# Head sums, centring and lora products of an RWKV-7 block: split F32R products in place of plain F32 ones

## The chip, the cores and the metric

The kernel runs on one core of a Trainium2 chip. The metric is the device time of one execution in microseconds. The page's names of the engines are used: PE is TensorE (PEld its weight loads), DVE is VectorE, ACT is ScalarE, POOL is GpSimd, SP is SyncE, whose queue issues most of the loads.

## The reference

One decoder block for 512 tokens of width 2048, batch 1, depth 1, all in float32. An adaLN-modulated RMS norm is projected by `w_in`; 1024 columns go to 16 RWKV-7 heads of 64, 1024 to a causal pooling mixer; both are joined by `w_out`, and a gated MLP with a causal convolution follows. The change is in the RWKV part:

```python
    r, k, v, xw, xa, xg = jnp.split(p, list(RWKV_SPLITS), axis=-1)     # p = p + mu * (shifted p - p)
    w = -jax.nn.softplus(-(w0 + jnp.tanh(xw) @ w2)) - 0.5               # lora, 64 wide
    a = jax.nn.sigmoid(a0 + xa @ a2)                                    # lora, 64 wide
    g = jax.nn.sigmoid(xg) @ g2                                         # gate, 160 wide
    kk = heads(k * k_k)
    kk = kk / jnp.maximum(jnp.sqrt(jnp.sum(kk * kk, axis=-1, keepdims=True)), L2_EPS)   # sum over a head
    k = k * (1.0 + (a - 1.0) * k_a)
    y = _wkv7_scan(r_h, decay, k_h, v_h, -kk, kk * a_h)                 # S = S*w + (S a) b + v k ; y = S r
    mean = jnp.mean(y, axis=-1, keepdims=True)                          # over a head
    var = jnp.mean(jnp.square(y - mean), axis=-1, keepdims=True)
    y = (y - mean) * lax.rsqrt(var + GN_EPS) * ln_w + ln_b
    bonus = jnp.sum(r_h * k_h * r_k, axis=-1, keepdims=True) * v_h      # sum over a head
    return (y + bonus) * g
```

## The kernel before

Features lie on the 128 partitions and the 512 tokens along the free dimension. The large products are split: a float32 operand x becomes `hi`, its value cast to F32R, and `lo = x - hi`, also F32R; `mm3` makes hi·hi + hi·lo + lo·hi out of three F32R products (L120 to L122). The cast is made by ScalarE and the subtraction by VectorE (`split_weights`, L113 and L115; `wsplit`, L855 and L857).

The stages: modulation and the first eight column tiles of `w_in` (tile `pf`); the recurrence; `w_out`; the MLP. In the recurrence the 16 heads are taken as 8 pairs of 128 partitions, and 512 tokens as 4 chunks of 128. For each pair there are three parts. `stage_a` makes decay and rates from the lora weights (L375, L376), a running sum along the tokens (a scan, L383), the norm of k (squares L397, head sum L399), the matrix of a chunk and part of its inverse (by VectorE, through DRAM), and the bonus (head sum L460, L462). `stage_b` finishes the inverse, as `y1` (upper rows) and `y2`. `stage_c` runs over the four chunks with the state `sbd`; in each, `R` is made (L553), then `U` out of `y1`, `y2` and `R` (L556 to L559); after the chunks come centring (L590, matrix `cent`), the variance (L594, `bmean`), the norm and the gate product (L602, L603). `bones`, `bmean` and `cent` are three constant 128x128 matrices in `hmat`; a product with one of them sums or averages over the 64 partitions of each head. All these products were plain F32.

Around them stand products that nobody waits for soon: `win_pair(p + 2)` projects r, k, v two pairs ahead (tile `mm`, 3 x 48 products, the results go to DRAM through `spill`), and `ada_rest` has VectorE multiply rows of `w_ada` (`war`, L351, 192 in all) for the later modulation.

The order on each engine is made by a scheduler from priorities (`hp()` puts the recurrence first) and free buffers of the pools; each engine then works its list in that order, and waits where something is not ready. A tile that has a tag takes one of the `bufs` buffers of that tag: `ring` has 7, `war` 3, `post` 2, `spill` 2.

Of the kernel before, what the change touches and what calls it, by code (L numbers as in the profile page):

```python
# [9 lines left out]
F32 = mybir.dt.float32  # L10
# [6 lines left out]
P = 128  # L17
T = 512
# [37 lines left out]
def block_kernel(ctx, tc, a, out, stop=None, dbg=None):  # L56
# [14 lines left out]
    hmat = tp.tile([P, 3, P], F32, tag="hmat", name="hmat")  # L71
    nc.sync.dma_start(hmat, a["cmat"][:, 2:5, :])
# [6 lines left out]
    scanm = tp.tile([P, NC, 129], F32, tag="scanm", name="scanm")  # L79
    nc.gpsimd.memset(scanm, 1.0)  # L80
    nc.gpsimd.memset(scanm[:, :, 0:1], 0.0)
    lanei = tp.tile([64, 16, 16], F32, tag="lanei", name="lanei")
    nc.sync.dma_start(lanei, a["lanei"][:, :, :])
# [93 lines left out]
    if True:  # L177
# [53 lines left out]
        if True:  # L231
# [5 lines left out]
            def ring(name):  # L237
                return ring16(name)[:, 16:]

            def ring16(name):  # L240
                return ra.tile([P, 16 + T], F32, tag="ring", name=name, bufs=7)


            xwa = ra.tile([P, T], F32, tag="xwa", name="xwa")
            xg1 = ra.tile([P, T], F32, tag="xg1", name="xg1")
            xg2 = ra.tile([P, T], F32, tag="xg2", name="xg2")
# [18 lines left out]
            S.activation(xg2, xg2, AF.Sigmoid)  # L265
# [67 lines left out]
    y1 = ra.tile([P, 8, 64], F32, tag="y1", name="y1")  # L333
    G.memset(y1[64:128], 0.0)
# [25 lines left out]
    def r8(t, n=64):  # L360
        return t[:, 0 : 8 * n].rearrange("p (s j) -> p s j", s=8)
# [3 lines left out]

    def stage_a(p, rkv):
        q = Pair()
        r, k, v = rkv
        lw = q.lw = ra.tile([P, 3, P], F32, tag="lw", name="lw", bufs=2)
        nc.sync.dma_start(lw, a["lora"][p, :, :, :])  # L370
# [4 lines left out]
        PE.matmul(psw, lw[0:64, 0, :], xwa[0:64, :], start=True, stop=True)  # L375
        PE.matmul(psal, lw[64:128, 0, :], xwa[64:128, :], start=True, stop=True)  # L376
# [6 lines left out]
        V.tensor_tensor_scan(cs[:, :, :].rearrange("p c t -> p (c t)"), scanm[:, :, :].rearrange("p c t -> p (c t)"),  # L383
                             sg[:, :, :].rearrange("p c t -> p (c t)"), 0.0, op0=ALU.mult, op1=ALU.add)
# [14 lines left out]
        PE.matmul(psn, bones, sq, start=True, stop=True)  # L399
# [868 lines left out]
```

## Time and profile before

| | |
|---|---|
| time, median of 3 runs | 2369.44 us (2361.89 to 2372.39) |
| profiled execution | 2368.65 us, its span 2366.9 us |
| busy: PE, DVE, ACT | 95%, 69%, 45% of the span |
| mean granted TensorE clock | 0.991 |
| recurrence | about 150 to 790 us of the span |

In the rows of the trace a shape such as "128*64" after the names is the part of TensorE's array that the instruction uses, in rows and columns, and "128x512 f32" is the output and its type; F32R operands are shown as f32 in products, and as fp32r in casts. Ends of products are modelled, so starts are what to compare. The page's digits are busy tenths of a slice of 1/40 of the span.

### The profile page before, as it was taken

To read this page: it belongs to the slowest core of one execution; us is meant where nothing else is said; L and a number is where in the kernel's file an instruction comes from. 1 tells how busy PE (TensorE), PEld (TensorE's weight loads), DVE (VectorE), ACT (ScalarE), POOL (GpSimd) and SP (SyncE) were. 2 spreads that over 40 slices of the span, in tenths; PEclk is the share of its full clock that TensorE was granted. 3 is DMA by queue.
4 is the path that set the end of the run, shared out by engine and by line. 5 is a ranking of instruction groups with operands and counts; after the bars stand their busy time and mean duration, and the time that the engine had idled before them with its cause. 6 is when DMAs were issued, how large, how long until landed. Compare 5 with 4: busy or idle time off the path is not lost.

```text
span 2366.9 us, 42831 instructions
## 1 busy us (share of the span) xinstructions
PE 2256.6 (95%) x17122; PEld 1960.0 (83%) x17122; DVE 1636.4 (69%) x2591; ACT 1067.4 (45%) x1501; POOL 126.0 (5%) x185
## 2 busy tenths in 40 slices
PE   3878999999999999999999999999999999999997
PEld 2655666666676789999999999999999888888897
DVE  6987677777765556788888877777777645353454
ACT  3235344445433345655555555555555522233353
POOL 0000000000000000010101000000000000110000
PEclk9999999999999999999999999999999999999998
DMA  9976655566655766598888877777776767664464
GB/s 340 339 227 181 165 151 157 156 171 178 164 143 154 268 199 192 178 282 250 227 246 233 243 208 199 198 197 199 199 197 186 237 213 269 228 209 118 123 185 156
DMA packets 226234, 483.06 MB, mean 204 GB/s; under 512 B 74545, under 2 KB 79601, under 8 KB 217841
## 3 DMA queue, kind: packets, MB, share of 16 engines
q1 hardware_dynamic: 206114, 413.21, 54.7%
q0 software_dynamic: 18864, 66.07, 13.6%
q8 instruction: 134, 2.20, 0.4%
q10 hardware_dynamic: 1056, 1.05, 0.1%
q14 instruction: 66, 0.54, 0.1%
HBM read 441.70 MB, written 38.54 MB: 203 GB/s over the span
## 4 chain that ended last, share of the span: by engine, by line
PE 75%; issue 10%; DVE 7%; DMA 4%; ACT 3%; SPq 1%; POOL 0%; POOLq 0%; DVEq 0%; ACTq 0%
PE b L122 18%; PE b L120 18%; PE b L121 18%; PE mm L121 4%; PE mm L122 4%; PE mm L120 4%; DVE jk L212 3%; DMA war<-ada 1%; PE pb L541 1%; PE pb L539 1%; DVE wlo L115 1%; DMA wrow<-wup 1%; DMA rkv<-sp 1%; PE pa L298 1%; DMA wraw<-wout 1%
## 5 line engine op out<-in xcount | busy, mean ns | idle before, releaser
L122 PE MATMUL b<-t,ulo 128*128 128x256 f32 x1408 | 397.2, 282 | 0.0
L120 PE MATMUL b<-t,uhi 128*128 128x256 f32 x1408 | 396.8, 282 | 0.0
L121 PE MATMUL b<-t,uhi 128*128 128x256 f32 x1408 | 396.7, 282 | 0.0
L122 PE MATMUL b<-act,ulo 128*128 128x512 f32 (+1 forms) x880 | 308.0, 350 | 0.0
L121 PE MATMUL b<-act,uhi 128*128 128x512 f32 (+1 forms) x880 | 307.8, 350 | 0.0
L120 PE MATMUL b<-act,uhi 128*128 128x512 f32 (+1 forms) x880 | 307.7, 350 | 0.0
L120 PE MATMUL b<-y,uhi 128*128 128x256 f32 x1056 | 298.1, 282 | 2.6 <-ACT uhi L855 2.6
L122 PE MATMUL b<-y,ulo 128*128 128x256 f32 x1056 | 297.6, 282 | 0.6 <-DVE ulo L857 0.6
L121 PE MATMUL b<-y,uhi 128*128 128x256 f32 x1056 | 297.8, 282 | 0.0
L857 DVE TENSOR_TENSOR ulo<-wd,uhi 128x1024 fp32r<-128x1024 f32 (+1 forms) x120 | 136.3, 1136 | 215.9 <-ACT uhi L855 206.7
L120 PEld LDWEIGHTS b<-t,uhi 128*128 128x128 f32 x1408 | 266.9, 190 | 0.0
L122 PEld LDWEIGHTS b<-t,ulo 128*128 128x128 f32 x1408 | 266.9, 190 | 0.0
L121 PEld LDWEIGHTS b<-t,uhi 128*128 128x128 f32 x1408 | 266.8, 190 | 0.0
L113 ACT CAST whi<-wraw 128x512 fp32r<-128x512 f32 x236 | 144.9, 618 | 265.0 <-PE mm L121 117.1
L855 ACT CAST uhi<-wquart 128x1024 fp32r<-128x1024 f32 x156 | 163.8, 1050 | 203.8 <-PE b L121 177.5
L855 ACT CAST uhi<-wd 128x1024 fp32r<-128x1024 f32 (+1 forms) x120 | 117.3, 978 | 290.8 <-PE b L121 290.2
L857 DVE TENSOR_TENSOR ulo<-wquart,uhi 128x1024 fp32r<-128x1024 f32 x156 | 190.8, 1224 | 72.0 <-ACT uhi L855 72.0
L115 DVE TENSOR_TENSOR wlo<-wraw,whi 128x512 fp32r<-128x512 f32 x236 | 161.0, 687 | 88.6 <-ACT whi L113 81.6
L855 ACT CAST uhi<-r 128x1024 fp32r<-128x1024 f32 x132 | 138.6, 1050 | 163.7 <-PE b L121 162.2
L857 DVE TENSOR_TENSOR ulo<-r,uhi 128x1024 fp32r<-128x1024 f32 x132 | 161.2, 1221 | 62.4 <-ACT uhi L855 62.4
L120 PEld LDWEIGHTS b<-y,uhi 128*128 128x128 f32 x1056 | 200.2, 190 | 3.0 <-ACT uhi L855 3.0
L122 PEld LDWEIGHTS b<-y,ulo 128*128 128x128 f32 x1056 | 200.0, 189 | 0.8 <-DVE ulo L857 0.8
(315 smaller groups left out, 4699.1 us busy)
## 6 DMA issues: line engine op xcount, KB each, us to landing
wquart<-wup SPq DMA_DIRECT2D x176, 512.0 KB, 4.8
wa<-ada SPq DMA_DIRECT2D x48, 1024.0 KB, 7.1
war<-ada SPq DMA_DIRECT2D x192, 256.0 KB, 3.6
wd<-wdn SPq DMA_DIRECT2D x80, 512.0 KB, 3.9
wraw<-win SPq DMA_DIRECT2D x140, 256.0 KB, 4.0
wraw<-wout SPq DMA_DIRECT2D x96, 256.0 KB, 3.7
wquart<-wup POOLq DMA_DIRECT2D x44, 512.0 KB, 7.5
r<-wup SPq DMA_DIRECT2D x44, 512.0 KB, 4.4
```

The lines of the kernel that those rows point to most:

```text
L113: S.copy(hi, raw)
L115: eng.tensor_tensor(lo, raw, hi[:, :].bitcast(F32), op=ALU.subtract)
L120: PE.matmul(ps, wh, xh, start=start, stop=False, skip_group_check=more)
L121: PE.matmul(ps, wh, xl, start=False, stop=False, skip_group_check=more)
L122: return PE.matmul(ps, wl, xh, start=False, stop=stop, skip_group_check=more)
L212: V.scalar_tensor_tensor(jk, wa, 1.0, cb, op0=ALU.mult, op1=ALU.mult, accum_out=mod[:, j : j + 1])
L298: PE.matmul(ps, pw[:, i, d * P : (d + 1) * P], zs[i], start=i == 0, stop=i == 1)
L539: PE.matmul(pss[:, h, 0:128], bt[HS[h], cl], ar[HS[h], c, 1, :], start=True, stop=True)
L541: PE.matmul(pss[:, h, 128:384], kt[HS[h], cl], ar[HS[h], c, :, :], start=True, stop=True)
L855: S.copy(hi[:, 0:n], src)
L857: lo_of[0] = V.tensor_tensor(lo[:, 0:n], src, hi[:, 0:n].bitcast(F32), op=ALU.subtract)
```

## The change

The four head sums and the centring per pair become products of a split operand: `head_sums` casts its operand to `hi`, subtracts for `lo` and adds the two F32R products with the same constant matrix; `hmat` is cast to F32R once. (`y` is split likewise, ahead of `cent`.) The two lora products become three F32R products each, of split weights (`lsplit`) and a split `xwa`; the gate product becomes five, of which the last two hold the 32 columns that are left of `g2`: `xg3` keeps hi and lo of xg2 in two groups of 32 partitions, and the packed weights repeat theirs.

To make room, the scan along 516 columns becomes four of 129 without its mask `scanm`; `y1`, `x5`, `nl`, `lanei` and `xyl` share two tiles, `half1` and `half2`, the first two on partitions 0 to 63 and the others on 64 to 127; `y1` has no zero rows below it any more, and its product reads `R[0:64]`. `sqy` takes the buffer of `Tm`, the lora weights one of `war`, `xwa` and `xg1` those of `spill`, `xg2` one of `post`.

```diff
@@
     nc.sync.dma_start(cmat, a["cmat"][:, 0:2, :])
-    hmat = tp.tile([P, 3, P], F32, tag="hmat", name="hmat")
-    nc.sync.dma_start(hmat, a["cmat"][:, 2:5, :])
+
+    hmat = tp.tile([P, 3, P], F32R, tag="hmat", name="hmat")
+    hraw = wp.tile([P, WC], F32, tag="wraw", name="hraw", bufs=4)[:, 0 : 3 * P]
+    nc.sync.dma_start(hraw, a["cmat"][:, 2:5, :].rearrange("p i j -> p (i j)"))
+    S.copy(hmat[:, :, :].rearrange("p i j -> p (i j)"), hraw)
     ident, ones = (cmat[:, i, :] for i in range(2))
@@
     nc.sync.dma_start(mlev, a["mlev"][:, :, :])
-    scanm = tp.tile([P, NC, 129], F32, tag="scanm", name="scanm")
-    nc.gpsimd.memset(scanm, 1.0)
-    nc.gpsimd.memset(scanm[:, :, 0:1], 0.0)
-    lanei = tp.tile([64, 16, 16], F32, tag="lanei", name="lanei")
-    nc.sync.dma_start(lanei, a["lanei"][:, :, :])
     prec = tp.tile([P, 16], F32, tag="prec", name="prec")
@@
-            def ring(name):
-                return ring16(name)[:, 16:]
+            def ring(name, dt=F32):
+                return ring16(name, dt)[:, 16:]
-            def ring16(name):
-                return ra.tile([P, 16 + T], F32, tag="ring", name=name, bufs=7)
+            def ring16(name, dt=F32):
+                return ra.tile([P, 16 + T], dt, tag="ring", name=name, bufs=7)
-            xwa = ra.tile([P, T], F32, tag="xwa", name="xwa")
-            xg1 = ra.tile([P, T], F32, tag="xg1", name="xg1")
-            xg2 = ra.tile([P, T], F32, tag="xg2", name="xg2")
+            xwa = ra.tile([P, T], F32, tag="spill", name="xwa", bufs=2)
+            xg1 = ra.tile([P, T], F32, tag="spill", name="xg1", bufs=2)
+            xg2 = ra.tile([P, T], F32, tag="post", name="xg2", bufs=2)
             for i, t in enumerate((xwa, xg1, xg2)):
@@
             S.activation(xg1, xg1, AF.Sigmoid)
-            S.activation(xg2, xg2, AF.Sigmoid)
+            S.activation(xg2[0:64], xg2[0:64], AF.Sigmoid)
+
+            def split_in(t, name):
+                hi = ra.tile([P, T], F32R, tag=name + "h", name=name + "h")
+                lo = ra.tile([P, T], F32R, tag=name + "l", name=name + "l")
+                S.copy(hi, t)
+                V.tensor_tensor(lo, t, hi[:, :].bitcast(F32), op=ALU.subtract)
+                return hi, lo
+
+            xwh, xwl = split_in(xwa, "xwa")
+            xgh, xgl = split_in(xg1, "xg1")
+
+            xg3 = ra.tile([P, T], F32R, tag="xg3", name="xg3")
+            S.copy(xg3[0:64], xg2[0:64])
+            V.tensor_tensor(xg3[32:64], xg2[32:64], xg3[32:64].bitcast(F32), op=ALU.subtract)
             ps0ctx.close()
@@
     G.memset(xy, 0.0)
-    y1 = ra.tile([P, 8, 64], F32, tag="y1", name="y1")
-    G.memset(y1[64:128], 0.0)
+
+    half1 = ra.tile([P, T], F32, tag="half1", name="half1")
+    half2 = ra.tile([P, T], F32, tag="half2", name="half2")
+    y1 = half1[0:64].rearrange("p (s j) -> p s j", s=8)
+    x5 = half2[0:64].rearrange("p (s j) -> p s j", s=8)
+    nl = half1[64:128, 0:256].rearrange("p (i j) -> p i j", i=16)
+    lanei = half1[64:128, 256:512].rearrange("p (i j) -> p i j", i=16)
+    xyl = half2[64:128].rearrange("p (w i j) -> p w i j", w=2, i=16)
+    nc.sync.dma_start(lanei, a["lanei"][:, :, :])
     dxz = [tc.dram_tile([32, 2, 32, 32], F32, name=f"dxz{i}") for i in range(2)]
@@
+    def head_sums(ps, m, t, hi, lo):
+
+        S.copy(hi, t)
+        V.tensor_tensor(lo, t, hi.bitcast(F32), op=ALU.subtract)
+        PE.matmul(ps, m, hi, start=True, stop=False)
+        PE.matmul(ps, m, lo, start=False, stop=True)
+
     def stage_a(p, rkv):
@@
         r, k, v = rkv
-        lw = q.lw = ra.tile([P, 3, P], F32, tag="lw", name="lw", bufs=2)
-        nc.sync.dma_start(lw, a["lora"][p, :, :, :])
+        lraw = ra.tile([P, T], F32, tag="war", name="lraw", bufs=3)[:, 0 : 3 * P]
+        nc.sync.dma_start(lraw, a["lora"][p, :, :, :].rearrange("p i j -> p (i j)"))
+
+        def lsplit(lo, hi, tag, bufs):
+            h = ra.tile([P, hi - lo], F32R, tag=tag + "h", name=tag + "h", bufs=bufs)
+            l = ra.tile([P, hi - lo], F32R, tag=tag + "l", name=tag + "l", bufs=bufs)
+            S.copy(h, lraw[:, lo:hi])
+            V.tensor_tensor(l, lraw[:, lo:hi], h[:, :].bitcast(F32), op=ALU.subtract)
+            return h, l
+
+        lah, lal = lsplit(0, P, "lwa", 1)
@@
         psal = atile()
-        PE.matmul(psw, lw[0:64, 0, :], xwa[0:64, :], start=True, stop=True)
-        PE.matmul(psal, lw[64:128, 0, :], xwa[64:128, :], start=True, stop=True)
+        for n, (l, x) in enumerate(((lah, xwh), (lah, xwl), (lal, xwh))):
+            for h, ps in enumerate((psw, psal)):
+                PE.matmul(ps, l[HS[h], :], x[HS[h], :], start=n == 0, stop=n == 2)
+        q.lg = lsplit(P, 3 * P, "lwg", 2)
         sg = ra.tile([P, NC, 129], F32, tag="sg", name="sg", bufs=2)
@@
         cs = ra.tile([P, NC, 129], F32, tag="sg", name="cs", bufs=2)
-        V.tensor_tensor_scan(cs[:, :, :].rearrange("p c t -> p (c t)"), scanm[:, :, :].rearrange("p c t -> p (c t)"),
-                             sg[:, :, :].rearrange("p c t -> p (c t)"), 0.0, op0=ALU.mult, op1=ALU.add)
+        for c in range(NC):
+            V.tensor_tensor_scan(cs[:, c, :], ones[:, 0:1].to_broadcast([P, 129]), sg[:, c, :], 0.0, op0=ALU.mult,
+                                 op1=ALU.add)
         mid = ra.tile([P, NC, 1], F32, tag="mid", name="mid", bufs=2)
@@
         psn = atile()
-        PE.matmul(psn, bones, sq, start=True, stop=True)
+        head_sums(psn, bones, sq, ring("sqh", F32R), ring("sql", F32R))
         inv = ring("inv")
@@
             nc.sync.dma_start(dn[8 * b : 8 * b + 8, :, :].rearrange("s i j -> i s j"), nt[BS[b], :, BS[b]])
-        nl = ra.tile([64, 16, 16], F32, tag="nl", name="nl")
         for e in range(2):
             es = slice(16 * e, 16 * e + 16)
-            nc.sync.dma_start(nl[32 * e : 32 * e + 32, :, :], dn[0:32, es, es])
-        xyl = ra.tile([64, 2, 16, 16], F32, tag="xyl", name="xyl")
+            nc.sync.dma_start(half1[64 + 32 * e : 96 + 32 * e, 0:256].rearrange("p (i j) -> p i j", i=16), dn[0:32, es, es])
         V.tensor_add(xyl[:, 1, :, :], nl, lanei)
-        prod = ra.tile([64, 64], F32, tag="prod", name="prod")
+        prod = ra.tile([P, 64], F32, tag="prod", name="prod")[64:128]
         for s in range(1, 15):
@@
         psb = atile()
-        PE.matmul(psb, bones, k2, start=True, stop=True)
+        head_sums(psb, bones, k2, ring("k2h", F32R), ring("k2l", F32R))
         bv = q.bv = ra.tile([P, T], F32, tag="bv", name="bv", bufs=2)
@@
             PE.matmul(pY[0:64, o], Tm[0:64, s, :], Y[0:64, s, :], start=True, stop=True)
-        x5 = ra.tile([64, 8, 64], F32, tag="x5", name="x5")
         V.tensor_add(x5, X[0:64], r8(pX)[0:64])
@@
         V.tensor_add(y2[64:128], Y[64:128], r8(pY)[64:128])
-        V.tensor_add(y1[0:64], Y[0:64], r8(pY)[0:64])
+        V.tensor_add(y1, Y[0:64], r8(pY)[0:64])
@@
                 s = 2 * c + h
-                PE.matmul(pc[0:64, 128 + 64 * h : 192 + 64 * h], y1[:, s, :], R[:, HS[h]], start=True, stop=True)
+                PE.matmul(pc[0:64, 128 + 64 * h : 192 + 64 * h], y1[:, s, :], R[0:64, HS[h]], start=True, stop=True)
                 PE.matmul(pc[64:128, 128 + 64 * h : 192 + 64 * h], y2[:, s, :], R[:, HS[h]], start=True, stop=True)
@@
-        y = ra.tile([P, T], F32, tag="post", name="y", bufs=2)
-        S.copy(y, py)
+        yh = ra.tile([P, T], F32R, tag="post", name="yh", bufs=2)
+        S.copy(yh, py)
+        yl = ra.tile([P, T], F32R, tag="post", name="yl", bufs=2)
+        V.tensor_tensor(yl, py, yh[:, :].bitcast(F32), op=ALU.subtract)
         pyc = ctile("y")
-        PE.matmul(pyc, cent, y, start=True, stop=True)
-        sq = ra.tile([P, T], F32, tag="post", name="sqy", bufs=2)
+        PE.matmul(pyc, cent, yh, start=True, stop=False)
+        PE.matmul(pyc, cent, yl, start=False, stop=True)
+        sq = ra.tile([P, T], F32, tag="Tm", name="sqy")
         S.activation(sq, pyc, AF.Square)
         pv = ctile("ch")
-        PE.matmul(pv, bmean, sq, start=True, stop=True)
+        head_sums(pv, bmean, sq, *(ra.tile([P, T], F32R, tag="post", name=n, bufs=2)[:, :] for n in ("sqh", "sql")))
         rs = ra.tile([P, T], F32, tag="post", name="rs", bufs=2)
@@
         pg = ctile("ch")
-        PE.matmul(pg, q.lw[:, 1, :], xg1, start=True, stop=False)
-        PE.matmul(pg, q.lw[0:32, 2, :], xg2[0:32, :], start=False, stop=True)
+        lh, ll = q.lg
+        PE.matmul(pg, lh[:, 0:P], xgh, start=True, stop=False)
+        PE.matmul(pg, lh[:, 0:P], xgl, start=False, stop=False)
+        PE.matmul(pg, ll[:, 0:P], xgh, start=False, stop=False)
+        PE.matmul(pg, lh[0:64, P:], xg3[0:64, :], start=False, stop=False)
+        PE.matmul(pg, ll[0:32, P:], xg3[0:32, :], start=False, stop=True)
         V.tensor_mul(rs, rs, pg)
@@
     mu[: 3360] = A(mu_shift[0])
+    mu[3360:3392] = mu[3328:3360]
     put("mu", mu)
@@
     lora[:, 0:32, 2, :] = A(g2[0])[128:].reshape(32, NP, P).transpose(1, 0, 2)
+    lora[:, 32:64, 2, :] = lora[:, 0:32, 2, :]
     o["lora"] = lora
```

The change moves instructions, since the scheduler makes a new order. On TensorE, a chunk of `stage_c`: L556 (`y1`) and L557 (`y2`) before, in the last place of the names the tile that is multiplied with R:

```order
L539 MATMUL pb<-ar,bt 128x128
L556 MATMUL ch<-R,y_1091 64x64
L557 MATMUL ch<-R,y_2325 64x64
L556 MATMUL ch<-R,y_1091 64x64
L557 MATMUL ch<-R,y_2325 64x64
L539 MATMUL pb<-ar,bt 128x128
L541 MATMUL pb<-ar,kt 128x256
L562 MATMUL ch<-tok 64x64 x2
L564 MATMUL ch<-U,tok 64x64 x2
```

and after, where they are L591 (`half1`, which holds `y1`) and L592:

```order
L574 MATMUL pb<-ar,bt 128x128
L591 MATMUL ch<-R,half_1099 64x64
L592 MATMUL ch<-R,y_1426 64x64
L591 MATMUL ch<-R,half_1099 64x64
L592 MATMUL ch<-R,y_1426 64x64
L574 MATMUL pb<-ar,bt 128x128
L576 MATMUL pb<-ar,kt 128x256 x2
L597 MATMUL ch<-tok 64x64 x2
L599 MATMUL ch<-U,tok 64x64 x2
```

The order is the same; what the rows don't show is that L591 now takes 64 rows of R, and L592 128 as before.

On TensorE, the end of a pair: the variance (L594) and the gate (L602, L603) before, with L120 to L122 as the projection of a later pair:

```order
L594 MATMUL ch<-sqy,hmat 128x512
L120 MATMUL mm<-ah_229,whi 128x512
L121 MATMUL mm<-al_230,whi 128x512
L122 MATMUL mm<-ah_229,wlo 128x512
L120 MATMUL mm<-ah_281,whi 128x512
L602 MATMUL ch<-xg_1055,lw 128x512
L603 MATMUL ch<-xg_1056,lw 128x512
```

and after, where the variance is L389 and L390, and the gate begins with L641 (two more products of it, L644 and L645, follow):

```order
L389 MATMUL ch<-sqh,hmat 128x512
L119 MATMUL mm<-al_955,whi 128x512
L120 MATMUL mm<-ah_954,wlo 128x512
L118 MATMUL mm<-ah_1006,whi 128x512
L390 MATMUL ch<-sql,hmat 128x512
L119 MATMUL mm<-al_1007,whi 128x512
L120 MATMUL mm<-ah_1006,wlo 128x512
L118 MATMUL mm<-ah_226,whi 128x512
L119 MATMUL mm<-al_227,whi 128x512
L641 MATMUL ch<-xg1h,lwgh 128x512
L642 MATMUL ch<-xg1l,lwgh 128x512
L643 MATMUL ch<-xg1h,lwgl 128x512
```

Three products of the projection now stand between the high and the low part of the variance, and four between that and the gate, as before.

On ScalarE, the start of the recurrence: activations of xwa and xg, then the casts of the projection's weights (L113), before:

```order
L262 COPY upad<-pf_217 128x512
L264 ACT_TABLE_LOAD
L264 ACTIVATE xg_1055<-xg_1055 128x512
L265 ACTIVATE xg_1056<-xg_1056 128x512
L113 CAST whi<-wraw 128x512 x5
```

and after, where L268 and L276 are the casts of the split inputs and L111 those of the projection's weights:

```order
L262 ACT_TABLE_LOAD
L262 ACTIVATE xg_1052<-xg_1052 128x512
L263 ACTIVATE xg_1053<-xg_1053 64x512
L268 CAST xwah<-xwa 128x512
L268 CAST xg1h<-xg_1052 128x512
L276 CAST xg_1086<-xg_1053 64x512
L111 CAST whi<-wraw 128x512 x5
```

Three casts came ahead of the projection's; three more, of the lora weights (L401), stand further up between the shifts of `rkv`.

More of the change, by code (lines that the diff above doesn't have):

```diff
@@ L1212, in pack @@
         w = 32 if n == "T2" else P
-        blk[i, :, :, :w] = wi[:, starts[n] : starts[n] + w].reshape(KT, P, w)
+        for o_ in (0, w) if n == "T2" else (0,):
+            blk[i, :, :, o_ : o_ + w] = wi[:, starts[n] : starts[n] + w].reshape(KT, P, w)
     o["win0"] = C(blk[:8].transpose(1, 2, 0, 3)).reshape(KT, P, 8 * P)
```

## The prediction

> **What bounds the kernel now.** I read the page's sections 1 and 2 first, then TensorE's own waits between 150 and 790 us (the stage that the change touches), then busy time by stretch, and last the timeline of TensorE around the products in question.
>
> ```profile
> span 2366.9 us, 42831 instructions
> PE 2256.6 (95%) x17122; PEld 1960.0 (83%) x17122; DVE 1636.4 (69%) x2591; ACT 1067.4 (45%) x1501; POOL 126.0 (5%) x185
> PE   3878999999999999999999999999999999999997
> DVE  6987677777765556788888877777777645353454
> ...
> 348.00:412.00 64.00, 61.67 (x644) 41.80 (x644) 47.94 (x124) 32.12 (x47) 0.00 (x0) 1.00 0.56 160
> ...
> 400.00:500.00 100.00, 96.38 (x1008) 66.35 (x1009) 72.63 (x186) 51.11 (x75) 0.00 (x0) 1.00 0.64 173
> 500.00:600.00 100.00, 96.79 (x985) 67.37 (x983) 78.52 (x201) 43.30 (x69) 0.00 (x0) 1.00 0.60 165
> sum 640.00, PE 606.35 PEld 421.28 DVE 460.98 ACT 280.38 POOL 1.76; mean PE 86.62 PEld 60.18 DVE 65.85 ACT 40.05 POOL 0.25
> ```
>
> The last four rows are stretches of the recurrence (length; then busy us of PE, PEld, DVE, ACT), the first of them about one pair of heads long, and the sum over 150 to 790 us. TensorE is busy 96 to 97 of 100 us there, VectorE 72 to 79, ScalarE 43 to 51. So a microsecond taken from TensorE's list is a microsecond of the stage, as long as the other two deliver in time; an addition on VectorE or ScalarE costs only where TensorE comes to wait for it. Such waits are few now:
>
> ```profile
> PE pb L483 <- issue: 5.8, 4, 1.6
> PE mm L122 <- DVE wlo L115: 4.5, 3, 3.5
> PE mm L120 <- ACT whi L113: 3.7, 2, 2.3
> PE pa L399 <- ACT sq L397: 3.4, 3, 1.5
> ...
> PE ch L602 <- ACT rs L596: 1.7, 2, 1.3
> ...
> PE pa L460 <- DVE nt L420: 0.8, 2, 0.5
> ```
>
> (us in total, times, longest.) The other five groups of products that the change rewrites (L375, L376, L590, L594, L603) are not in this list: TensorE never stood idle for them.
>
> **The four head sums (L399, L460, L590, L594).** Each is one plain F32 product of 512 columns per pair of heads, inside a stream of F32R products (mm):
>
> ```profile
> 470.01 1.02 PE L590 MATMUL y<-y,hmat 128*128 128x512 f32 x2
> 470.47 0.79 PE L122 MATMUL mm<-ah,wlo 128*128 128x512 f32 x1
> 471.10 0.40 PE L120 MATMUL mm<-ah,whi 128*128 128x512 f32 x1
> 471.33 0.39 PE L121 MATMUL mm<-al,whi 128*128 128x512 f32 x1
> ```
>
> From start to start one F32R product takes 0.23 us (471.10 to 471.33). From 470.01 to 471.10 stand one head sum and one mm, so the head sum holds TensorE 1.09 - 0.23 = 0.86 us. Two F32R products take 0.46. Saved: 0.40 x 4 sums x 8 pairs = 13 us.
>
> **The gate product (L602, L603).**
>
> ```profile
> 473.37 0.40 PE L120 MATMUL mm<-ah,whi 128*128 128x512 f32 x1
> 473.72 1.12 PE L602 MATMUL ch<-xg,lw 128*128 128x512 f32 x2
> 474.78 1.12 PE L603 MATMUL ch<-xg,lw 32*128 32x512 f32 x2
> 475.83 0.50 PE L121 MATMUL mm<-al,whi 128*128 128x512 f32 x1
> 476.17 0.39 PE L122 MATMUL mm<-ah,wlo 128*128 128x512 f32 x1
> ```
>
> From 473.37 to 476.17 there are 2.80 us, less two mm of 0.23: 2.34 for the pair. Five F32R products are 1.15, and three changes of tile shape stand in them (128, 64, 32 rows and back; the shape of the array that an instruction uses is the column "32*128"). A change costs 0.1 us: see the next fence. So 1.45, saved 0.9 x 8 = 7 us.
>
> **The lora products (L375, L376).**
>
> ```profile
> 481.18 0.39 PE L120 MATMUL mm<-ah,whi 128*128 128x512 f32 x1
> 481.50 0.69 PE L375 MATMUL pa<-xwa,lw 64*128 64x512 f32 x1
> 481.51 0.69 PE L376 MATMUL pa<-xwa,lw 64*128 64x512 f32 x1
> ...
> 482.56 0.50 PE L121 MATMUL mm<-al,whi 128*128 128x512 f32 x1
> 482.89 0.39 PE L122 MATMUL mm<-ah,wlo 128*128 128x512 f32 x1
> ```
>
> The step into another shape is 0.32 and the step after the return 0.33 where 0.23 is the norm: 0.1 us a change. The two products start together, one on each half of the rows, and with both changes cost 482.89 - 481.18 - 0.46 = 1.25 us. In the new order the six F32R products mostly stand three and three on one half, so I count them one after another: 1.38 + 0.2 = 1.6. Where other work separates the two today they cost up to twice the 1.06 between 481.50 and 482.56, the latter in three of eight pairs by the order. Five times +0.35 and three times -0.6 is about nothing: 0, between -3 and +3.
>
> **What moves against it: y1 times R (L556, L557).** y1 lost its zero lower half, and its product now reads R[0:64], 64 rows; its partner with y2 still reads 128. Before, both have one shape:
>
> ```profile
> 450.38 0.27 PE L556 MATMUL ch<-R,y 128*64 128x64 f32 x1
> 450.38 0.27 PE L557 MATMUL ch<-R,y 128*64 128x64 f32 x1
> ...
> 450.54 0.22 PE L556 MATMUL ch<-R,y 128*64 128x64 f32 x1
> ...
> 450.60 0.22 PE L556 MATMUL ch<-R,y 128*64 128x64 f32 x1
> ...
> 450.76 0.70 PE L541 MATMUL pb<-ar,kt 64*128 64x256 f32 x4
> ```
>
> They run side by side in two column halves, in steps of 0.06 us; the four of a chunk are through in 0.38. In the new order they alternate 64*64, 128*64, 64*64, 128*64: three changes more (0.3) and no partner to run beside (four steps of 0.06 more, 0.24). That is +0.5 us in each of 32 chunks: +16 us. No row has these two shapes next to each other. Lower bound 0 (shapes mix freely); upper, if each change exposes a whole weight load of 0.2, 32 x (0.6 + 0.24) = 27. I take 16, because every change of shape in the quoted rows costs its 0.1.
>
> The Trainium skill, "TensorEngine Tiling (Array Packing)", section Tiling Modes, says that "Changing tiling mode (not just tile) drains the TensorE". By it the mix cannot be free, and the trace agrees with 0.1 us at each change of shape shown.
>
> Counted over the whole order, neighbours on TensorE that differ in shape go from 402 to 528: 96 by y1, 8 in the gate product, some 22 because small products are cut up more: 22 x 0.1 = +2.
>
> **What is added on the other engines.**
>
> ```profile
> L115 DVE TENSOR_TENSOR wlo<-wraw,whi 128x512 fp32r<-128x512 f32 x102 | 69.4, 684 | 30.4 <-ACT whi L113 27.3 <-PE mm L122 2.0 <-DMA war<-ada 0.5
> L383 DVE TENSOR_TENSOR_SCAN cs<-scanm,sg 128x516 f32<-128x516 f32 x8 | 9.8, 1228 | 6.8 <-ACT sg L379 6.8
> L351 DVE SCALAR_TENSOR_TENSOR war<-war,cq 128x512 f32<-128x512 f32 x174 | 117.0, 681 | 24.5 <-DMA war<-ada 24.2
> L113 ACT CAST whi<-wraw 128x512 fp32r<-128x512 f32 x100 | 61.2, 617 | 128.0 <-PE mm L121 100.8 <-issue 9.6 <-DMA war<-ada 6.1
> ```
>
> Per pair VectorE gets four subtractions like L115 (2.7 us), the two low halves of the lora weights (384 columns, about 0.5) and four scans of 129 for one of 516, at most some tenths more than 1.23: 3.5 us. ScalarE gets three casts like L113 and the weights' casts: 2.4. Busy shares of VectorE of 73 to 79% become about 80 to 85%, ScalarE's stay near 50%. As work this is hidden under TensorE; what shows is each new place where TensorE's queue stands still until a cast and then a subtraction are done, with all mm products behind it. There are seven per pair (low part of all four sums, high part of two of them, low lora weights): 56. Nearest rows: the five head-sum and gate products wait 3.4 + 0.8 + 1.7 us over 40 times, 0.15 each; L399, which has the same kind of chain ahead, 0.43. So 8 to 24 us, and not below zero, since a wait gives nothing back. I take 0.2 each, 11 us, near the mean, as most sit among mm products that were put there to cover them.
>
> At the start (150 to 200 us) ScalarE gets, ahead of the first whi casts, three casts of xwa, xg1, xg2 and three of lora weights, some 2.8 us, and VectorE three subtractions. The two longest waits above (3.5 and 2.3 us) are those mm products waiting there for wlo and whi: they get longer by about what is put ahead: +3.5 (0 to 5). lraw shares the three war buffers, so the ada rows come later: 26 of 192 instead of 18 are left after the last pair. At 0.7 us each that is 5 us more VectorE beside the last products, of which I count 2 (0 to 8). hmat's cast, the moved lanei load and the missing memsets lie under the first loads, ahead of any product: 0. sqy in Tm's buffer and the shared halves add waits among products of neighbouring pairs, which mm covers.
>
> **The sum.** -13 - 7 + 0 + 16 + 2 + 11 + 3.5 + 2 = +14.5. The profiled execution took 2368.65 us (span 2366.9), 0.8 below the median 2369.44, so the sum gives 2383.
>
> **The rivals.** *Faster: unlike shapes cost nothing and the waits stay covered.* Then y1's 16 and the 11 go: -12.5, 2356. For it: all other engines have slack, and the order was made to cover waits. Against it: 0.1 us at each quoted change. Decided at y1: under 0.1 us per chunk. Chance 0.17. *Same: the shapes cost as said, the waits are covered*: 14.5 - 11 = +3.5, 2372. For it: L590 and L594 wait for nothing today though ScalarE runs between them. Chance 0.28. *Much slower: VectorE becomes the bound.* Of 64 us, about a pair, it works 48 and idles 16 on others' results; if that idle time stays while its work grows by 3.5, a pair takes 67.5: 8 x 3.5 = 28 and the start's 3.5, 2400. For it: ada rows that wait for their loads (L351, 24 us in all) stand in the same queue. Against it: the idle time is mostly waiting for TensorE. Chance 0.10. *Forecast*: 0.45, own range 2376 to 2392.
>
> **How the numbers follow.** About 0.5% (12 us) is what a measurement of this kernel can tell from no change: 2357.6 to 2381.3 is "same". The forecast's own range lies to four fifths above it: slower 0.36 + 0.10 = 0.46; same 0.28 + 0.09 = 0.37; faster 0.17. The range runs from the faster rival with a little less start, 2354, to the bound by VectorE, 2402.
>
> **What would show it.** Right: L591 and L592 start one after the other, 0.2 us apart, and a chunk's four take 0.8 to 0.9 us; a head sum 0.46 between mm products; TensorE's waits name L390 and L628 for VectorE, some 10 us more in all; everything after the first output-projection product is unchanged. Wrong: L591 and L592 still start together; or PE's idle time from 150 to 790 us doesn't grow; or it grows by over 25 us with VectorE above 90%.

## The result and the profile after

The changed kernel takes 2405.34 us (median of 4 runs, 2403.2 to 2405.91) against 2368.57 us (4 runs, 2361.89 to 2372.39): a ratio of 1.0157, 95% interval 1.0133 to 1.0181. That is slower, as forecast, but by 37 us where 14.5 were forecast, and above the forecast's range of 2376 to 2392. Its profiled execution took 2405.78 us. (One profiled execution further down, that of kernel 3, was of a slower kind, 2834.57 us at a mean granted clock of 0.723, so that kernel's other four times are used and its trace is not.) From the page of the changed kernel:

```profile
span 2404.0 us, 43037 instructions
PE 2279.8 (95%) x17146; PEld 1989.9 (83%) x17146; DVE 1686.9 (70%) x2666; ACT 1079.8 (45%) x1540; POOL 125.0 (5%) x182
PE   4778999999999999999999999999999999999997
PEclk9989999999989999999999999999999999999998
```

The busy shares read as before: nothing in them says 37 us. The clock row does: the slices of 60 us from 120 and from 661 us have an 8, where before there was a 9 all through the recurrence. The first output-projection product stands here in the timelines of before and of the changed kernel (start, duration, what; in brackets the idle time ahead of it and what ended it):

```profile
778.82 0.39 PE L120 MATMUL pb<-ah,whi 128*128 128x512 f32 x1
```

```profile
812.29 0.50 PE L118 MATMUL pb<-ah,whi 128*128 128x512 f32 x1 [3.17 <-ACT whi L111]
```

So 33.5 of the 37 us lie ahead of it. The rest of the span differs by 3.6 us, of which two more stretches of half clock there explain most. To see where they went I added up TensorE's time from 150 us to that product, from start to start of consecutive products and without the idle time ahead of the next ("work"; the same idle times make the list of waits). Half of what lies in a stretch of granted clock 0.5 is counted apart ("half clock"). In us:

| | y1, y2 x R | mm | head sums | gate | lora | other small | half clock | idle |
|---|---|---|---|---|---|---|---|---|
| before | 12.2 | 340.2 | 20.7 | 16.9 | 11.6 | 186.6 | 7.2 | 31.4 |
| after | 32.8 | 332.1 | 19.1 | 13.6 | 11.7 | 186.7 | 18.1 | 48.2 |

The products with R cost 20.6 us more; mm, head sums and gate give back 13.0; idle time grows by 16.8; and half clock by 10.9, for which the forecast had no term. (These add up to 35.5 with the small rest, as 2 us of idle time just behind 150 us in the kernel before stand in no column.) TensorE's waits, 150 to 870 us:

```profile
PE pa L455 <- DVE bt L447: 8.7, 3, 3.9
PE pb L519 <- issue: 7.0, 3, 3.8
PE pb L118 <- ACT whi L111: 4.0, 2, 3.2
PE pb L532 <- DVE xy L523: 3.3, 3, 1.9
PE pa L389 <- DVE nt L458: 2.8, 3, 1.3
PE ch L390 <- DVE sql L388: 2.5, 4, 1.3
PE ch L641 <- ACT rs L634: 2.5, 4, 1.2
```

and three of the same places before:

```profile
PE pa L417 <- DVE bt L409: 3.7, 3, 2.0
PE pb L120 <- ACT whi L113: 1.0, 1, 1.0
PE pb L496 <- DVE xy L487: 0.7, 1, 0.7
```

The new handshakes (L389, L390, L641) are there, but over half of the growth is at products that the change doesn't touch: bt (8.7 for 3.7), xy (3.3 for 0.7), the first whi of the output projection (4.0 for 1.0). VectorE comes late with the first two, ScalarE with the third. What such lateness costs is seen best at 656 to 684 us (timeline, then three stretches with busy PE, PEld, DVE, ACT, POOL and the clock):

```profile
658.82 0.40 PE L119 MATMUL mm<-al,whi 128*128 128x512 f32 x1
661.09 1.97 PE L532 MATMUL pb<-xy,nt 64*64 64x64 f32 x32 [1.87 <-DVE xy L523]
666.94 2.08 PE L455 MATMUL pa<-ar,bt 64*128 64x128 f32 x16 [3.88 <-DVE bt L447]
...
678.34 0.79 PE L120 MATMUL mm<-ah,wlo 128*128 128x512 f32 x1
...
680.21 0.46 PE L118 MATMUL mm<-ah,whi 128*128 128x512 f32 x1
680.52 0.39 PE L119 MATMUL mm<-al,whi 128*128 128x512 f32 x1
640.00:660.00 20.00, 18.37 (x260) 13.90 (x258) 12.54 (x27) 9.08 (x14) 0.00 (x0) 1.00 0.66 190
660.00:680.00 20.00, 14.34 (x114) 11.40 (x115) 15.67 (x33) 5.59 (x9) 0.00 (x0) 0.50 0.62 178
680.00:700.00 20.00, 20.00 (x161) 13.36 (x160) 13.79 (x43) 4.52 (x10) 0.00 (x0) 0.99 0.48 146
```

For 19.5 us no mm product stands in TensorE's list; 6.4 us are idle, and the clock is 0.50 from 660 until mm products are back (their duration falls from 0.79 to 0.39). This one place holds 6 us of idle time, and up to 10 us were lost to half clock there.

The products with R, in a chunk of the changed kernel:

```profile
457.93 0.48 PE L574 MATMUL pb<-ar,bt 64*128 64x128 f32 x2
458.34 0.32 PE L591 MATMUL ch<-R,half 64*64 64x64 f32 x2
458.60 0.33 PE L592 MATMUL ch<-R,y 128*64 128x64 f32 x2
458.86 0.33 PE L591 MATMUL ch<-R,half 64*64 64x64 f32 x2
459.11 0.33 PE L592 MATMUL ch<-R,y 128*64 128x64 f32 x2
459.37 0.37 PE L574 MATMUL pb<-ar,bt 64*128 64x128 f32 x1
```

One after the other, 0.26 apart, 1.03 us for the four where 0.38 stood before. (Each plain F32 product stands as two instructions in the trace, hence x2.)

### The profile page after: what moved, and what is told of

Same layout as the page of the kernel before. It is cut to its first block, busy times and chain, and to the rows that moved or that the text cites. A ratio compares the mean times of both kernels' runs of the same rounds, so it can differ in the third digit from the quotient of the medians.

```text
span 2404.0 us, 43037 instructions
## 1 busy us (share of the span) xinstructions
PE 2279.8 (95%) x17146; PEld 1989.9 (83%) x17146; DVE 1686.9 (70%) x2666; ACT 1079.8 (45%) x1540; POOL 125.0 (5%) x182
## 4 chain that ended last, share of the span: by engine, by line
PE 67%; issue 9%; DVE 4%; DMA 3%; ACT 2%; POOL 0%; POOLq 0%; DVEq 0%; SPq 0%; ACTq 0%
PE b L120 17%; PE b L118 17%; PE b L119 17%; PE mm L118 2%; PE mm L120 2%; PE mm L119 2%; DMA wrow<-wup 1%; DVE war L370 1%; PE pb L576 1%; DMA war<-ada 1%; PE pb L574 1%; DVE wlo L113 1%; PE ch L592 0%; DMA wraw<-wout 0%; PE ch L591 0%
## 5 line engine op out<-in xcount | busy, mean ns | idle before, releaser
L120 PE MATMUL b<-t,ulo 128*128 128x256 f32 x1408 | 397.3, 282 | 0.0
L120 PE MATMUL b<-act,ulo 128*128 128x512 f32 (+1 forms) x880 | 308.0, 350 | 0.0
L120 PE MATMUL b<-y,ulo 128*128 128x256 f32 x1056 | 297.3, 282 | 0.3 <-DVE ulo L899 0.3
L111 ACT CAST whi<-wraw 128x512 fp32r<-128x512 f32 x236 | 145.1, 618 | 276.6 <-PE mm L119 122.6
L120 PEld LDWEIGHTS b<-t,ulo 128*128 128x128 f32 x1408 | 266.9, 190 | 0.0
L113 DVE TENSOR_TENSOR wlo<-wraw,whi 128x512 fp32r<-128x512 f32 x236 | 160.2, 687 | 72.8 <-ACT whi L111 70.3
L120 PEld LDWEIGHTS b<-y,ulo 128*128 128x128 f32 x1056 | 199.3, 189 | 0.5 <-DVE ulo L899 0.5
```

What stands on the lines that cost most here:

```text
L111: S.copy(hi, raw)
L113: eng.tensor_tensor(lo, raw, hi[:, :].bitcast(F32), op=ALU.subtract)
L120: return PE.matmul(ps, wl, xh, start=False, stop=stop, skip_group_check=more)
```

## The experiments

Each time is a median, with the ratio to the kernel before on the same chip (2364 to 2368 us) and its interval. "Work", "half clock" and "idle" are the sums of the table above, of the profiled execution, which can lie some us off the median; before has 588.2, 7.2 and 31.4, after 596.0, 18.1 and 48.2.

**1. The mix of shapes alone.**

```diff
-  PE.matmul(pc[0:64, ...], y1[:, s, :], R[:, HS[h]], ...)
+  PE.matmul(pc[0:64, ...], y1[0:64, s, :], R[0:64, HS[h]], ...)
```

> The kernel before with one edit: y1's product reads only the upper 64 rows, y1[0:64] and R[0:64], as the changed kernel does. Nothing else differs, and every engine has the same instructions in the same order. Theory (the mix of shapes has its own price on TensorE): the traces of the two kernels give 12.2 us for the 256 products with R before and 32.8 us after, so this kernel should take about 2369 + 20 = 2389 us, with L556 and L557 starting one after the other and a chunk's four at about 1.0 us in place of 0.38. Rival (the mix only fills time in which TensorE would have waited, and the loss comes from waits): within 5 us of 2369.

2383.97 us, 1.0076 (1.0062 to 1.0089), 17 us slower. The order is that of before on every engine, so this is the price of the mix: of the changes of shape and of the lost side by side together, which it doesn't tell apart. TensorE's groups, with busy time and mean (before: 14.3 us and 234 ns each, but side by side):

```profile
L557 PE MATMUL ch<-R,y 128*64 128x64 f32 x128 | 21.0, 246 | 0.0
L556 PE MATMUL ch<-R,y 64*64 64x64 f32 x128 | 20.8, 243 | 0.0
```

Work is 607.3, 19.1 more; idle 29.0.

**2. The mix undone in the changed kernel.** y1 is a full tile, with zeros below. To make room, `nl` and `lanei` go to partitions 0 to 63; `xyl` and `prod` stay on 64 to 127.

```diff
-  PE.matmul(pc[0:64, ...], y1[:, s, :], R[0:64, HS[h]], ...)
+  PE.matmul(pc[0:64, ...], y1[:, s, :], R[:, HS[h]], ...)     # y1: 128 rows; x5 = y2[0:64]
```

> The changed kernel with one part undone: y1 is a full tile of 128 rows with zeros below again, and its product reads all of R (x5 takes y2's upper rows, nl and lanei the upper half of half2, to make room). The order on TensorE, ScalarE and SyncE is the same as in the changed kernel. Theory (mix 20.6 us, waits 16.8 us more, half-clock stretches 14 us more, split products 13 us less): 2405 - 20 = 2385 us, still 16 slower than before. Rival 1 (the products with R were hidden beside VectorE's work, so that the waits grow by what they give back): 2400 or more. Rival 2 (the mix caused the half-clock stretches too): about 2371.

2388.47 us, 1.0093 (1.008 to 1.0106): 17 us back by the medians, 15 by the ratios, with the order kept, near the 20 of the theory (work 578.3, idle 51.3, half clock 19.0). Work is now 10 us below that of before, and the kernel 21 us above it.

**3 and 4. Half of the split products each**, both with full y1: first lora and gate alone, then the head sums alone.

```diff
-  head_sums(psn, bones, sq, ring("sqh", F32R), ring("sql", F32R))     # 3: all four
+  PE.matmul(psn, bones, sq, start=True, stop=True)
-  PE.matmul(pg, lh[:, 0:P], xgh, ...)                                 # 4: lora and gate
+  PE.matmul(pg, q.lw[:, 1, :], xg1, ...)
```

> As the last one (full y1), and the four head sums plain F32 products again; split are only the lora and the gate products. Theory (the waits and the clock come from the subtractions of the head sums in VectorE's queue, 2.7 of the 3.2 us that VectorE gets per pair): the gate's -3 and some 5 us of waits and clock remain: 2371 us, and waits for VectorE's bt and xy back to about what they were. Rival (they come from the lora weights, which are now split at the head of each pair, out of a buffer of the ada rows): 2380 or more.

> As the last but one (full y1), and the lora and gate products plain F32 again; split are only the four head sums. Theory (waits from the head sums' subtractions): head sums 9.5 us less, waits and clock some 26 more: about 2386 us. Rival (waits from the lora weights): 2369 - 9.5 + 3 = about 2362, faster than before.

2384.07 us, 1.0073 (1.006 to 1.0086), and 2387.95 us, 1.0093 (1.0078 to 1.0108). The first fits the rival, the second the theory, and together they fit neither: each half alone loses nearly as much as both. That points at something that both share.

**5 and 6. What they share: the room.** First the scan in four pieces alone in the kernel before, then the changed kernel with full y1 and no split product.

```diff
-  V.tensor_tensor_scan(cs[...p (c t)], scanm, sg[...p (c t)], 0.0, ...)
+  for c in range(NC):
+      V.tensor_tensor_scan(cs[:, c, :], ones[:, 0:1].to_broadcast([P, 129]), sg[:, c, :], 0.0, ...)
```

> The kernel before with one edit: the scan of 516 columns is made as four of 129, as in the changed kernel; everything else, the mask's room included, stays. The edit moves the order of instructions: the list of TensorE has the matrix of bt and ar (L417) behind eight mm products more at one place, and 764 of its 14,262 rows stand elsewhere. In the two traces the four pieces take 1.65 us for 1.23, 0.42 x 8 = 3.4 us of VectorE in all. Theory 1 (new after the runs so far, in which either half of the split products alone costs as much as both: the waits and the half-clock stretches come with the order that the scan in four pieces brings): 2380 to 2390 us, with stretches of half clock in the recurrence that the kernel before doesn't have. Theory 2 (they come from the subtractions that the split products add): 2367 to 2371 us.

> The changed kernel with full y1 and with all head sums, lora and gate products plain F32 again: what is left of the change is the room that it makes (scan in four, x5 in y2, xyl, nl and lanei in one tile). Theory 1 (order brought by the scan): 2380 to 2390 us. Theory 2 (subtractions): 2367 to 2371 us.

2364.36 us, 0.9987 (0.9976 to 0.9997), slightly faster, so theory 1 fell for the scan. The room costs: 2380.99 us, 1.0063 (1.0044 to 1.0082). The two have the same instructions in the same order on TensorE, VectorE and ScalarE, and on SyncE but for lanei's load. Still VectorE takes 1.1 to 1.8 us longer for each pair's small chain (prod, xyl), 3.0 at the first. Its timeline there, of before, and of the changed kernel:

```profile
335.84 0.20 DVE L435 TENSOR_TENSOR prod<-xyl,nl 64x50 f32<-64x50 f32 x1
335.96 0.68 DVE L351 SCALAR_TENSOR_TENSOR war<-war,cq 128x512 f32<-128x512 f32 x1
336.57 0.08 DVE L351 DVE_READ_ACCUMULATOR war<-war,cq 128x1 f32 x1
336.57 0.20 DVE L437 TENSOR_TENSOR xyl<-xyl,prod 64x50 f32<-64x50 f32 x1
```

```profile
234.07 0.20 DVE L471 TENSOR_TENSOR prod<-half,half 64x44 f32<-64x44 f32 x1
234.30 0.69 DVE L370 SCALAR_TENSOR_TENSOR war<-war,cq 128x512 f32<-128x512 f32 x1
234.92 0.08 DVE L370 DVE_READ_ACCUMULATOR war<-war,cq 128x1 f32 x1
235.03 0.20 DVE L473 TENSOR_TENSOR half<-half,prod 64x44 f32<-64x44 f32 x1
```

The durations agree. But from one small step to the next there are 0.73 us before and 0.96 after: on partitions 64 to 127 neither the instruction behind the small one (0.23 for 0.12) nor the small one itself (0.11 behind the accumulator's read, where it was 0.00) overlaps the instruction ahead. Kernels 5 and 6 differ likewise, 0.72 and 0.96 us in the median.

**7 and 8. Two more guesses on the head sums**: the scan in one piece again, and ten ring buffers for seven.

```diff
+  V.tensor_tensor_scan(cs[...p (c t)], scanm, sg[...p (c t)], 0.0, ...)                     # 7
-  return ra.tile([P, 16 + T], dt, tag="ring", name=name, bufs=7)
+  return ra.tile([P, 16 + T], dt, tag="ring", name=name, bufs=10)     # 8
```

> Full y1, the four head sums split, lora and gate plain F32, and the scan in one piece with its mask again. Theory 1 (order brought by the scan): 2367 less the 7 us that head sums and the mm products next to them give back, plus up to 5 for new waits: 2360 to 2366. Theory 2 (subtractions): 2383 to 2390, as with the scan in four (2388).

> Full y1, the four head sums split, lora and gate plain F32, the scan in four, and ten buffers in place of seven for the tag ring, from which a pair now takes ten. Rival theory 3 (the casts and subtractions of a head sum wait for ring buffers, and so do those behind them): 2370 to 2378. Theory 1 (order brought by the scan) and theory 2 (subtractions): about the 2388 of seven buffers.

2387.86 us, 1.0089 (1.0073 to 1.0106), and 2390.85 us, 1.0098 (1.0081 to 1.0115): neither is the cause.

**9. The upper rows alone.**

```diff
-  nl = ra.tile([64, 16, 16], F32, tag="nl", name="nl")
+  nl = ra.tile([P, 16, 16], F32, tag="nl", name="nl")[64:128]     # lanei, xyl and prod alike
```

> The kernel before with one edit: nl, lanei, xyl and prod, on which VectorE works 28 small steps per pair (L435, L437), lie on partitions 64 to 127 in place of 0 to 63, as in the changed kernel. Every engine has the same instructions in the same order as before. Theory 4 (new: the step of VectorE into and out of such an instruction is 0.12 us longer on the upper rows; from the traces, war to small step to war takes 0.73 us on the lower rows and 0.97 on the upper ones, 0.24 x 28 x 8 = 54 us of VectorE's time, which no busy share shows, and TensorE pays where it waits for VectorE): 2378 to 2386 us. Rival (the difference between the kernel with the room made and the one with the scan alone, which have the same order, comes from lanei's load, which was moved behind others and shifts every later load to another queue): 2367 us.

2376.63 us, 1.0046 (1.0032 to 1.0061): 11 us slower, with every instruction in its old place. VectorE's timeline has the longer steps, 0.98 us from prod to xyl:

```profile
335.85 0.21 DVE L435 TENSOR_TENSOR prod<-xyl,nl 64x56 f32<-64x56 f32 x1
336.10 0.69 DVE L351 SCALAR_TENSOR_TENSOR war<-war,cq 128x512 f32<-128x512 f32 x1
336.71 0.08 DVE L351 DVE_READ_ACCUMULATOR war<-war,cq 128x1 f32 x1
336.83 0.21 DVE L437 TENSOR_TENSOR xyl<-xyl,prod 64x56 f32<-64x56 f32 x1
```

Shown, then, though a little smaller than expected. From the first prod to the last xyl the eight chains take 158 us in all, for 147 before: 11 us longer, not the 54 that the expectation counted. And of the 17 us between kernels 5 and 6 this leaves 6 unexplained. The Trainium skill, "VectorE: DVE Perf Modes", section "Two Vector instructions with no wait between them", has the rule, as a model: an instruction whose inputs or output start in another group of 32 partitions than those of the instructions ahead of it starts only when these have finished. The trace agrees, with 0.11 to 0.13 us at each change.

**10 to 12. The lower rows again, with full y1**: all split products, head sums alone, lora and gate alone.

```diff
-  prod = ra.tile([P, 64], F32, tag="prod", name="prod")[64:128]
+  prod = ra.tile([P, 64], F32, tag="prod", name="prod")[0:64]     # xyl = half2[0:64]; nl in x4's buffer
```

> The whole change with two parts undone: y1 is a full tile again, and nl, xyl and prod lie on partitions 0 to 63 again (nl takes the buffer of x4, x5 the upper rows of y2, lanei half of half2). All split products stay. Theory 4 (mix of shapes and upper rows are the loss): 2367 - 13 for the split products - 3 for the scan, plus 5 to 10 for new waits: 2356 to 2362 us, faster than before. Theory 2 (the subtractions are the loss): 2380 to 2388.

> As the last one, with lora and gate plain F32: only the head sums are split, on the lower rows. Theory 4: 2364 - 7 plus up to 5: 2357 to 2362. Theory 2: 2380 to 2388, as with the upper rows.

> As the last but one, with the head sums plain F32: only lora and gate are split, on the lower rows. Theory 4: 2364 - 3 plus up to 3: 2361 to 2364. Theory 2 or the rival of the lora weights: 2375 or more.

2382.62 us, 1.0069 (1.0051 to 1.0088); 2381.13 us, 1.0055 (1.0042 to 1.0069); 2368.84 us, 1.0015 (1.0005 to 1.0025). Against the ratios 1.0093, 1.0093 and 1.0073 on the upper rows (kernels 2, 4 and 3), these give 6, 9 and 14 us back. Of the three pairs, 4 and 11 have the same order on TensorE, VectorE and ScalarE, 2 and 10 have not. Lora and gate are 3 us from before; the head sums still lose 13 to 16, so theory 4 held for a part only.

**13 to 15. Is it their subtractions?** The low part left out; the subtractions on GpSimd; the same with all split products.

```diff
-  V.tensor_tensor(lo, t, hi.bitcast(F32), op=ALU.subtract)
-  PE.matmul(ps, m, hi, start=True, stop=False)
-  PE.matmul(ps, m, lo, start=False, stop=True)
+  PE.matmul(ps, m, hi, start=True, stop=True)                     # 13
+  G.tensor_tensor(lo, t, hi.bitcast(F32), op=ALU.subtract)        # 14 and 15, products as they were
```

> The head sums on the lower rows (2381 us) with their low part left out: a head sum is one F32R product of the cast operand, no subtraction and no second product, so the sums are less exact than the reference's. VectorE loses 4 x 0.68 = 2.7 us per pair, TensorE 0.23 x 32 = 7 us. Theory 5 (the loss of the head sums is VectorE being late, at one stretch near 650 us above all, where bt is waited for 4.5 us and the clock then stays at half for 17 us of small products): the stretch goes, 2381 - 7 - 15 = about 2359. Theory 6 (the cast alone, as one more step between ScalarE and TensorE, brings the order with that stretch): about 2374.

> The head sums on the lower rows (2381 us) with three of the four subtractions per pair on GpSimd, which has no work in the recurrence, in place of VectorE (that of y stays, as it reads TensorE's result). Theory 5 (VectorE late): 2364 to 2372, if GpSimd takes less than some 2 us each. Theory 6 (order brought by the cast): 2376 to 2384.

> All split products on the lower rows (2383 us) with the same three subtractions on GpSimd. Theory 5: 2364 to 2372, as lora and gate alone cost 3 us over before and the head sums give back 7. Theory 6: 2378 to 2386.

2378.27 us, 1.004 (1.0028 to 1.0052); 2382.62 us, 1.0056 (1.0039 to 1.0073); 2391.02 us, 1.0098 (1.0085 to 1.0112). GpSimd takes 1.4 to 2.2 us for a subtraction, where VectorE takes 0.68. Kernel 13 has no subtraction, 15 us less work than kernel 11 (563.5), and yet 10 us more idle (47.2) and as much half clock (24.5). So VectorE's added work is at most a small part of the cause: 3 us came back where 2.7 us of VectorE's time a pair and 15 us of TensorE's were left out.

**16 to 18. Is it TensorE's time that counts?** The head sums in one F32R product each, without an added step per sum (`hmat` is cast once, and `k2r` takes one more ring buffer per pair); the same with the scan in four; and that with each product done three times.

```diff
-  sq = ring("sq")                                                 # k2, y and sqy alike
+  sq = ring("sq", F32R)
   S.activation(sq, k, AF.Square, scale=col("kk", p))
-  PE.matmul(psn, bones, sq, start=True, stop=True)
+  for i in range(3):                                              # 18 only
+      PE.matmul(psn, bones, sq, start=True, stop=True)
```

> The kernel before with the four head sums made in one F32R product each, without any added step: the instruction that writes the operand (square, copy, product) writes it as F32R itself, and there is no low part, so the sums are less exact than the reference's; hmat is cast once. TensorE's work falls by (0.68 - 0.23) x 32 = 14 us, VectorE and ScalarE get nothing. Theory 6 (the additional cast and subtraction per sum bring the order that loses): 2366 - 14 = 2352 us. Theory 7 (new: TensorE's time that is given back in this stage is no time of the stage, as it goes into waits for the chain through the other engines, and gaps of over half a window of 3.41 us bring stretches of half clock besides): 2362 to 2376, with idle time and half clock above the 31 and 7 us of before by as much as the work falls.

> As the last one, with the scan in four pieces, which alone took 3 us off. Theory 6: about 2350 us. Theory 7: 2360 to 2376.

> The last kernel (2380 us) with each head sum's one product done three times over, into the same buffer with the same operands: useless work that gives TensorE back the 0.69 us that a plain F32 sum took (0.23 x 3), and nothing else. Every other order than before's is a new order too. Theory 7 (TensorE's time given back in this stage is worth nothing, and its gaps bring half clock): with more work on TensorE the time does not rise, and falls towards the 2364 us of plain F32 sums: 2362 to 2376. Theory 6, now as the plain counting of TensorE's work: 2380 + 0.46 x 32 = 2395. Theory 8 (each new order of the scheduler lies some 5 to 20 us over the order of before, whatever the work): 2370 to 2388, with gaps and half clock as many as in the last kernel.

2371.11 us, 1.0027 (1.0014 to 1.004); 2380.46 us, 1.0062 (1.0039 to 1.0085); 2382.75 us, 1.0063 (1.0049 to 1.0077). The groups of k's sum, of before, of 16 and of 18 (busy us, mean ns, idle ahead):

```profile
L460 PE MATMUL pa<-k,hmat 128*128 128x512 f32 x16 | 9.6, 683 | 0.8 <-DVE nt L420 0.8
```

```profile
L463 PE MATMUL pa<-k2r,hmat 128*128 128x512 f32 x8 | 3.9, 489 | 0.4 <-DVE nt L422 0.4
```

```profile
L465 PE MATMUL pa<-k2r,hmat 128*128 128x512 f32 x24 | 9.2, 444 | 0.4 <-DVE nt L423 0.4
```

| | time | profiled | stage ends | work | half clock | idle |
|---|---|---|---|---|---|---|
| before | 2364 to 2369 | 2369 | 778.8 | 588.2 | 7.2 | 31.4 |
| 5, scan in four | 2364 | 2362 | 772.1 | 586.1 | 7.4 | 28.5 |
| 12, lora and gate, lower rows | 2369 | 2374 | 775.6 | 583.8 | 9.0 | 32.7 |
| 16, sums direct | 2371 | 2376 | 779.4 | 568.9 | 18.4 | 41.7 |
| 17, sums direct, scan in four | 2380 | 2388 | 789.9 | 566.5 | 26.3 | 44.6 |
| 11, head sums split, lower rows | 2381 | 2383 | 790.8 | 579.0 | 24.4 | 36.9 |
| 10, all split, lower rows | 2383 | 2393 | 794.9 | 570.0 | 30.7 | 43.6 |
| 18, sums three times | 2383 | 2384 | 795.1 | 583.7 | 15.7 | 44.7 |

("Stage ends" is the start of the first output-projection product in the profiled execution.) Kernel 16 took 19 us off TensorE. Its stage ends where that of before does, 779.4 for 778.8: the 19 us have turned into 10 more of idle time and 11 more of half clock. What its profiled execution loses lies behind the stage, 6.6 us, of which 3.2 are half clock and 2.3 idle time. For these sums, then, TensorE's time is not the stage's time. For the products with R it nearly was: kernels 1 and 2, in which the order stays, paid and regained 15 to 17 us. Whether the kept order or the place of the products makes the difference, no run here separates. Kernel 18 put 17 us of useless work back into kernel 17: 2 us slower by the medians, which is within the spread of 17 (2371.7 to 2387.69), and a stage that ends 5 us later; idle time unchanged, half clock 10.6 us less. So plain counting (theory 6) is wrong by 12 us; but the time did not fall to 2364 as theory 7 had it, and theory 8 gave the time, though not the half clock. Rewritten head sums come with a new order each time, and each such order has 37 to 51 us of idle time (kernel 6, with the old sums, has 39). Why they wait more is not settled: every edit of these products moves the order, and a run with the new products in the old order was not made. Kernel 5 is the fastest of all.

## Why the prediction was right and wrong

- **"A microsecond taken from TensorE's list is a microsecond of the stage, as long as the other two deliver in time."** This step failed, for the head sums above all. The split products took 13.0 us (9.7 of head sums and the mm beside them, where 13 were forecast, and 3.3 of the gate, where 7 were) off the list, and the runs show such time not coming back: kernels 10, 11, 13 and 16 have 9 to 25 us less work than before and are 7 to 17 us slower; in 16 idle time and half clock took the place of the 19 us. For the products with R the same step held (kernels 1 and 2). The share of 97% busy, full of mm products that were put where others wait, doesn't say that TensorE sets the end; that this is why the time didn't come back is a reading that no run tests.
- **Half clock** had no term: 10.9 us, and some 3 after the recurrence. Waits were priced by their own length only.
- **The shared halves** were counted at nothing, as waits that mm covers. Their price came by VectorE's longer steps on upper rows: 11 us alone (kernel 9), 6 to 14 in the others. Nothing in busy times shows it, since the durations stay.
- **y1 times R** was right: the products start one after the other, 1.03 us a chunk (0.8 to 0.9 forecast), 20.6 us of TensorE's time and 15 to 17 us of the kernel's, for 16. The step from one to the next, 0.26 us, is larger than what 0.1 a change and no partner beside it add up to; how it is made up is not shown.
- **New waits, start and tail**, 11 + 3.5 + 2: idle time grew by 16.8, so the sum held, but by luck, as the places did not. Head sums and gate wait 12.7 us for 5.9; the rest is bt, xy and the first weights of the output projection, which was not "unchanged", as it begins with a wait of 3.17.
- **Lora** 0: 11.7 for 11.6. Right, though with some luck: the same products take 14.5 in kernel 12.
- **The rival of VectorE as the bound** had the size (2400) but not the cause: VectorE is 69 to 80% busy between 200 and 800 us here, and taking the subtractions away changed 3 us (kernel 13).
- **The chances**: of the forecast's range of 16 us, two thirds lie above 2381.3, not four fifths, so an even weight would have given slower 0.30 of it and not 0.36.

The 37 us along the runs, by the ratios: the mix 15 (from the changed kernel to 2, order kept), the upper rows 6 on top of the rest (from 2 to 10; 11 alone with the order kept, kernel 9), and 16 that kernel 10 still loses, of which the cause stays open. They add up because each run starts from the one before, so the sum proves nothing.

## What to carry to other kernels

A busy engine full of filler (products that nobody waits for soon) need not be the bound: before pricing a gain on it, ask whether anything at the end of the stage waits for the time it gives back. Take the start partitions of small VectorE steps and the shape of neighbouring products as part of an edit's price, even where the edit only saves room. And price a wait that leaves TensorE idle for more than half of a 3.41 us window with the half-clock stretch behind it.

## What the hardware showed

Half clock follows a busy share, on a fixed grid: stretches at clock 0.5 start on a grid of 3.41 us. Over 19 traces, 200 to 850 us, windows at full clock with TensorE busy under 0.4 were followed by half clock in 54 of 54 cases, at 0.4 to 0.5 in 18 of 23, at 0.5 to 0.7 in 22 of 134, above that in 3 of 3248. And small products lift it badly: of windows at half clock that were at least 0.8 busy, 82 of 86 with four or more products of 128x512 were followed by full clock, but 18 of 65 with fewer. The Trainium skill, "TensorE: Matmul & The Clock Gate", Part 1, states a free-running window of some 3.4 us, the half rate, and an idle window as the condition. The window and the rate agree; of the condition the traces differ, as a window that was less than half busy was enough.
